# The output projection by seven products on halves, with six of eight blocks finished by an accumulating transfer

## The chip, the cores and the metric

The kernel runs on one core of one Trainium2 chip. The metric is the device time of one execution in microseconds, as the median over runs. The engines of the core are TensorE (PE, with its weight loads in a row of their own, PEld), VectorE (DVE), ScalarE (ACT), GpSimd (POOL) and SyncE (SP). SP and POOL issue the transfers: SP through a hardware queue (q1), POOL through a software queue (q0), which alone can add to what stands at the destination.

## The reference, cut to what matters

One layer on x of 1024 positions by 1024 channels, float32:

```
h = x @ w_in + b_in                       # -> xa, za, xb, zb, ga, gb
ya = RG_LRU(causal_conv4(xa)) * silu(za)
yb = MultiScalePool(xb) * silu(zb)
merged = sigmoid(ga) * (ya @ w_proj_a) + sigmoid(gb) * (yb @ w_proj_b)
y = merged @ w_out + b_out
out = LayerNorm(alpha * x + y, ln_gain, ln_bias)      # alpha = 2 ** 0.25
```

The last two lines are the output projection and the norm. The norm takes mean and variance over the 1024 channels of a position, multiplies with the gain and adds the bias.

## The kernel before, in words

Each float32 operand of a matmul is split into a high and a low part (`split`: a ScalarE copy to the matmul's type, and a DVE subtraction), and each product is three matmuls: high by high, high by low, low by high. A matmul takes 128 by 128 weights and 512 columns into one of eight PSUM banks (`bank`).

The stages follow one another: the input projection in 22 groups (`Group`, kinds A, B and G), then the merge (`steps`, seven products on halves for each of the branches a and b), then the output projection. The input projection and the merge already use seven products on halves of the operands instead of eight. The sums of halves that the merge needs are made in device memory (DRAM) by transfers of POOL: `summed` queues a copy of 1 MB and then adds (`add_to`), as jobs in a list, and `run_jobs` takes some jobs off that list after each group, behind a small POOL copy (`paced`) that waits for that group's seventh product. Names: t1 to t4 are sums of the branch results ya and yb (t1b is the first for branch b), p1 to p4 sums of weights (p1a to p4a, p1b to p4b). The merge reads them back through SP: xa1r, wa1r and so on are its raw operands for branch a, product 1; xb6r is branch b, product 6.

The output projection of before (lines 1338 to 1398) is plain: for each of eight blocks of 128 positions and each of two halves of 512 output channels, one bank takes eight inner blocks by three passes (`o_mm`); DVE adds the bank to z, which holds alpha * x + b_out (`o_evac`), and takes the statistics of each half (`bn_stats`). When both halves of a block are done, `o_norm` makes mean and variance, the root on ScalarE, and two DVE scalings for each half, the second of which also adds the bias of the norm, and SP stores the block. The last bank is cut into two pieces of 256 columns. `split_m` splits the merged operand as it becomes ready, `load_wo` and `cast_wo` bring the weights.

The order of each engine's instructions is not that of the code. `Plan` records all operations, gives each a due time from a cost and from who needs it, and lays them out by a simulated clock: PE and POOL keep the order of the code, DVE, ScalarE and SP take what is ready and due first (line 359 on), and hold an instruction back if a more urgent one comes soon (line 361). Every instruction is emitted by line 389, so the profile names this one line and is read by tile names.

Of the kernel before, what the change touches and what calls it, by code (L numbers as in the profile page):

```python
# [16 lines left out]
P = 128  # L17
# [144 lines left out]
class Plan:  # L162
# [22 lines left out]
    def add(self, name, eng, op, args, kw):  # L185
# [6 lines left out]
        t.ins = refs[1:] if t.outs else refs  # L192
        t.deps, t.users, t.new = set(), [], []
# [61 lines left out]
    def order(self):  # L255
# [26 lines left out]
        state = {"table": None, "SP": 0.0, "ACT": 0.0, "POOL": 0.0, "pe": 0}  # L282
# [17 lines left out]
        def begin(t, now):  # L300
# [4 lines left out]
            t.start = now  # L305
            free[t.eng] = now + t.time
# [21 lines left out]
        while done < len(T):  # L328
            moved = True
            while moved:  # L330
# [10 lines left out]
                for e in ("ACT", "DVE", "SP", "POOL"):  # L341
# [60 lines left out]
def layer_kernel(ctx: ExitStack, tc: tile.TileContext, xq, x, w_in, par, wg, w_pool, wpa, wpb, w_out, rows, out):  # L402
# [33 lines left out]

    HALF = [slice(0, H), slice(H, S)]
# [289 lines left out]
    def a_gates(c, xc, xh, xl, sz):  # L727
# [388 lines left out]
    for i in range(1, len(order)):  # L1116
# [51 lines left out]
        if i >= 2:  # L1168
            run_jobs(1 if kind == "A" else 2, i, g.t7)
# [63 lines left out]
    sums, mh, ml = {}, {}, {}  # L1233
    HOMES = {2: (kt, kt), 5: (kt, xt), 4: (xt, rt), 3: (xt, xt)}
# [4 lines left out]
    def split_m(j, d, h):  # L1239
        if d % 2 == 0:  # L1240
            for k, t in enumerate((mh, ml)):
                f = HOMES[j][k]
                t[d // 2, h] = f(f"m{k}{d}{h}", F32R) if f is not kt else f(f"m{k}{d}{h}", F32R).rearrange("p (g s) -> p g s", g=2)
        sign = 1.0 if d < KQ else -1.0
        A.mul(of(mh, d, h), of(sums, d, h), sign)
        V.scalar_tensor_tensor(of(ml, d, h), of(sums, d, h), sign, of(mh, d, h).bitcast(F32), ALU.mult, ALU.subtract)

    wo = {}

    raw_wo = {}  # L1250


    def load_wo(e, p):
        raw_wo[e, p] = kt(f"wor{e}_{p}").rearrange("p (k n) -> p k n", k=2)
        nc.sync.dma_start(raw_wo[e, p], w_out[2 * p * P:2 * (p + 1) * P, e * H:(e + 1) * H].rearrange("(k p) n -> p k n", p=P))

    def cast_wo(e, p):
        h, l = ((wt if e == 0 else xt)(f"wo{t}{e}_{p}") for t in "hl")
        split(raw_wo.pop((e, p)), h, l)
        for k in range(2):  # L1260
            wo[e, 2 * p + k] = (h[:, k, :], l[:, k, :])
# [20 lines left out]
    for i, (n, j) in enumerate(steps):  # L1282
# [10 lines left out]
        for g in range(KQ):  # L1293
# [17 lines left out]
            if (n, j) in DONE:  # L1311
# [11 lines left out]
                else:  # L1323
                    V.tensor_tensor(u, t, sgs[i][g], ALU.mult)
                    V.tensor_tensor(of(sums, d, h), of(sums, d, h), u, ALU.add)
                    split_m(j, d, h)
            if (n, j, g) in CASTS:
                with nc.within(SOON):
                    cast_wo(0, CASTS.index((n, j, g)))
        if (n, j) in (("a", 4), ("b", 1)):  # L1330
            for p in range(2):
                load_wo(0, p if n == "a" else p + 2)
# [5 lines left out]
    for p in range(KQ):  # L1338
        load_wo(1, p)
        cast_wo(1, p)  # L1340
    rb = []
    for i in range(3):
        t = xt(f"row{i}", F32, (P, S))
        nc.sync.dma_start(t, rows[i:i + 1, :].to_broadcast((P, D)))
        rb.append(t)
    b_row, g_row, be_row = rb
    zt, stats = [], []
    for s in range(NK):
        t = xt(f"z{s}", F32, (P, S))
        nc.sync.dma_start(t, x[s * P:(s + 1) * P, :])  # L1350
        V.scalar_tensor_tensor(t, t, ALPHA, b_row, ALU.mult, ALU.add)
        zt.append(t)
        stats.append(const.tile([P, 4 if s == NK - 1 else 2, 6], F32, name=f"stats{s}"))
    eps = const.tile([P, 1], F32, name="eps")
    nc.gpsimd.memset(eps, EPS)

    def o_mm(ps, s, e, ks, sl=slice(0, H)):
        for k in ks:
            wh, wl = (w[:, sl] for w in wo[e, k])
# [94 lines left out]
```

## Time and profile before

| | |
|---|---|
| median of three runs | 754.5 us (754.29 to 754.6) |
| profiled execution | 754.04 us |
| its span, first to last instruction | 752.2 us |
| PE busy | 742.5 us, 3308 matmuls |
| DVE busy | 598.4 us |
| ACT busy | 432.2 us |
| POOL busy | 54.5 us |
| granted TensorE clock, mean of the span | 0.997 |
| moved by q1, by q0 | 99.43 MB, 35.65 MB |

Durations of single DVE and ACT rows include some time in which the next one has already started; two rows in sequence are closer together than the first one's duration. A POOL transfer's row is its issue, not its landing.

### The profile page before, as it was taken

How to read it: one execution, taken by the hardware profiler on the slowest of the kernel's cores; microseconds unless marked ns; L12 is line 12 of the kernel's file. 1: busy time of each engine (PE TensorE's matmuls, PEld its weight loads, DVE VectorE, ACT ScalarE, POOL GpSimd, SP SyncE). 2: the span in 40 equal slices, each digit the busy share in tenths (PEclk: the TensorE clock that was granted, in tenths of full speed). 3: DMA queues.
4: the chain of work that ended last, by engine and by line, in shares of the span. 5: the costliest groups of instructions: out<-in, count | busy, mean ns of one | idle time of the engine just before them, and what ended most of it. 6: DMA issues, size and time to landing. Idle time of an engine off the chain costs nothing.

```text
span 752.2 us, 8755 instructions
## 1 busy us (share of the span) xinstructions
PE 742.5 (99%) x3308; PEld 608.6 (81%) x3308; DVE 598.4 (80%) x740; ACT 432.2 (57%) x556; POOL 54.5 (7%) x101
## 2 busy tenths in 40 slices
PE   9999999999999999999999999999999999999996
PEld 6887888888788878878888888888888888888885
DVE  7898695959595969699977768779958896977587
ACT  7676969597787777788665444465543654230000
POOL 0160010101010100010011001000000000000000
PEclk9999999999999999999999999999999999999998
DMA  9146567657566647254278526898599996181022
GB/s 343 64 145 156 179 159 198 166 175 195 147 163 198 166 176 173 85 171 142 80 161 171 112 76 176 309 382 270 197 300 302 330 295 220 57 315 48 29 93 103
DMA packets 54730, 135.90 MB, mean 181 GB/s; under 512 B 3936, under 2 KB 7136, under 8 KB 54624
## 3 DMA queue, kind: packets, MB, share of 16 engines
q1 hardware_dynamic: 41248, 99.43, 37.9%
q0 software_dynamic: 12896, 35.65, 21.4%
q8 instruction: 26, 0.43, 0.2%
q10 hardware_dynamic: 544, 0.26, 0.1%
q14 instruction: 16, 0.13, 0.1%
HBM read 114.36 MB, written 56.62 MB: 227 GB/s over the span
## 4 chain that ended last, share of the span: by engine, by line
PE 95%; ACT 2%; DVE 1%; DMA 1%; issue 0%; DVEq 0%; ACTq 0%
PE ps_o L389 12%; PE a_B L389 11%; PE a_A L389 10%; PE a_G L389 10%; PE pa_a L389 6%; PE pa_b L389 6%; PE c_A L389 6%; PE c_B L389 5%; PE c_G L389 4%; PE ps_pool L389 3%; PE pc_b L389 3%; PE pc_a L389 3%; PE e_A L389 3%; PE ps_s L389 3%; PE e_G L389 3%; PE e_B L389 3%
## 5 line engine op out<-in xcount | busy, mean ns | idle before, releaser
L389 PE MATMUL ps_o<-woh,m 128*128 128x512 f32 (+1 forms) x272 | 80.5, 379 | 0.0
L389 ACT ACT_TABLE_LOAD x39 | 50.0, 1283 | 42.8 <-DVE mv L389 40.1
L389 PEld LDWEIGHTS ps_o<-woh,m 128*128 128x128 f32 x272 | 50.1, 188 | 10.1
L389 PE MATMUL ps_o<-wol,m 128*128 128x512 f32 (+1 forms) x136 | 51.5, 378 | 0.0
L389 DVE TENSOR_TENSOR i<-i,xc 128x1024 f32<-128x1024 f32 x8 | 9.8, 1225 | 38.6 <-ACT i L389 38.6
L389 POOL COPY paced<-pace 128x1 f32<-128x1 f32 x19 | 13.4, 706 | 259.6 <-ACT pace L389 259.6
L389 DVE SCALAR_TENSOR_TENSOR xc<-xp,par_sb,xc 128x1024 f32<-128x1024 f32 x24 | 30.8, 1282 | 0.5
L389 PEld LDWEIGHTS ps_o<-wol,m 128*128 128x128 f32 x136 | 25.6, 188 | 5.0
L389 DVE TENSOR_TENSOR z<-ps_o,z 128x512 f32<-128x512 f32 (+1 forms) x17 | 11.2, 659 | 18.8 <-PE ps_o L389 18.3
L389 PE MATMUL pa_a<-oh,oh 128*128 128x512 f32 x64 | 24.9, 389 | 0.0
L389 PE MATMUL pa_a<-oh,ol 128*128 128x512 f32 x64 | 24.9, 389 | 0.0
L389 PE MATMUL pa_a<-ol,oh 128*128 128x512 f32 x64 | 24.9, 389 | 0.0
L389 PE MATMUL pa_b<-oh,oh 128*128 128x512 f32 x64 | 24.9, 389 | 0.0
L389 PE MATMUL pa_b<-ol,oh 128*128 128x512 f32 x64 | 24.9, 389 | 0.0
L389 PE MATMUL pa_b<-oh,ol 128*128 128x512 f32 x64 | 24.9, 389 | 0.0
L389 ACT ACTIVATE m<-m 128x512 fp32r<-128x512 f32 x16 | 10.1, 632 | 25.3 <-DVE m L389 25.3
L389 ACT ACTIVATE i<-ps_g,par_sb 64x512 f32<-64x512 f32 x32 | 21.9, 685 | 3.3 <-DVE r L389 2.8
L389 ACT ACTIVATE sd<-mv,eps 128x1 f32<-128x1 f32 x8 | 2.4, 295 | 34.9 <-DVE mv L389 34.9
L389 ACT ACTIVATE r<-ps_g,par_sb 64x512 f32<-64x512 f32 x32 | 21.9, 684 | 0.5
L389 ACT ACTIVATE zb<-zb,par_sb 128x1024 f32<-128x1024 f32 (+1 forms) x16 | 14.9, 937 | 10.7 <-DVE zb L389 10.3
L389 PE MATMUL c_B<-x64h,wd_B 128*128 128x512 f32 x64 | 21.0, 389 | 0.0
L389 PE MATMUL c_A<-x64h,wd_A 128*128 128x512 f32 x64 | 21.0, 389 | 0.0
(435 smaller groups left out, 2380.9 us busy)
## 6 DMA issues: line engine op xcount, KB each, us to landing
sg<-sg SPq DMA_DIRECT2D x16, 512.0 KB, 3.6
ra_A<-in_w_in SPq DMA_DIRECT2D x8, 512.0 KB, 4.9
rb_A<-in_w_in SPq DMA_DIRECT2D x8, 512.0 KB, 3.8
ya<-r SPq DMA_DIRECT2D x8, 512.0 KB, 2.9
ra_B<-in_w_in SPq DMA_DIRECT2D x8, 512.0 KB, 3.4
rb_B<-in_w_in SPq DMA_DIRECT2D x8, 512.0 KB, 3.7
yb<-zb SPq DMA_DIRECT2D x8, 512.0 KB, 6.0
sgla<-sg SPq DMA_DIRECT2D x8, 512.0 KB, 6.3
```

The costliest lines, as they stand in the source:

```text
L389: getattr(getattr(nc, t.op[0]), t.op[1])(*a, **k)
```

## The change

The output projection becomes seven products on halves: the sums of halves of the weights are made by POOL transfers in DRAM (`output_sums`), those of the merged operand by DVE in SBUF (`o_sums`, `o_sum4`), and z takes each product as it is finished (`o_add`), in the order 1, 6, 7, 5, 3 and then, block by block, 4 and 2. x plus b_out / alpha is made in DRAM by POOL transfers (`biased_input`). For blocks 0 to 6 the sum of a row comes from a second output of the two last adds and the sum of squares from a second output of Square on ScalarE; only block 7 keeps `bn_stats`. For blocks 0 to 5 the output in DRAM is preset with the bias of the norm, and the scaled block is added to it by a POOL transfer. `run_jobs` takes two or three jobs a group instead of one or two. The planner adds PE's present lag to a due time where it decides to hold an instruction back. Removed: the loops of the projection of before,

```diff
-    for s in range(NK):
-        ps = bank(f"ps_o{s}_0")
-        o_mm(ps, s, 0, range(NK))
-        o_evac(ps, s, 0, H)
-    for s in range(NK - 1):
-        ps = bank(f"ps_o{s}_1")
-        o_mm(ps, s, 1, range(NK))
-        o_evac(ps, s, H, D)
-        o_norm(s)
-    s = NK - 1
-    for w in (slice(0, H // 2), slice(H // 2, H)):
-        ps = bank(f"ps_o{s}_1_{w.start}")[:, 0:H // 2]
-        o_mm(ps, s, 1, range(NK), w)
-        o_evac(ps, s, H + w.start, H + w.stop)
-    o_norm(s)
```

`split_m`, the bias row and `o_mm`. Added, cut to its core:

```diff
--- before.py
+++ after.py
@@ -190,6 +190,9 @@
         out = args[0]
         t.outs = [out] if isinstance(out, Ref) else []
         t.ins = refs[1:] if t.outs else refs
+        if isinstance(kw.get("accum_out"), Ref):
+            t.ins = [r for r in t.ins if r is not kw["accum_out"]]
+            t.outs.append(kw["accum_out"])
...
-                        if any(u.due < t.due and when < end and u.due < end - HOLD for when, u in soon):
+                        if any(u.due < t.due and when < end and u.due + state["lag"] < end - HOLD for when, u in soon):
...
+    def output_sums():
+        a11, a12, a21, a22 = (w_out[H * k:H * (k + 1), H * i:H * (i + 1)].rearrange("(q p) n -> q p n", p=P)
+                              for i in range(2) for k in (1, 0))
+        p1 = summed("p1o", a21, a22)
+        p3 = summed("p3o", a11, a21)
+        p2 = summed("p2o", a11, p1)
+        src["w", "o"] = {1: a11, 2: a12, 4: a22, 5: p1, 6: p2, 7: p3, 3: summed("p4o", a12, p2)}
+
+
+    xb_d = [dram.tile([2 * P, D], F32, tag=f"xb{i}", name=f"xb{i}") for i in range(4)]
+    bias_d = dram.tile([1, D], F32, tag="bias", name="bias")
+
+    def biased_input():
+        for sl in HALF:
+            t = epool.tile([1, H], F32, tag="e", name=f"bias_{sl.start}")
+            nc.sync.dma_start(t, rows[0:1, sl])
+            A.mul(t, t, 1.0 / ALPHA)
+            nc.sync.dma_start(bias_d[:, sl], t)
+        for i in (2, 3, 0, 1):
+            jobs.append(lambda i=i: nc.gpsimd.dma_start(xb_d[i], x[2 * P * i:2 * P * (i + 1), :]))
+            jobs.append(lambda i=i: add_to(xb_d[i], bias_d.to_broadcast((2 * P, D))))
...
             input_sums1("a")
+            output_sums()
         elif c == NK - 1:
             input_sums2("a")
+            biased_input()
...
-            run_jobs(1 if kind == "A" else 2, i, g.t7)
+            run_jobs(3 if kind == "B" else 2, i, g.t7)
...
+    def o_first(d):
+
+        p, i = divmod(d - KQ, 2)
+        if i == 0:
+            om.setdefault(1, []).append([kt(f"o1{n}{p}", F32R).rearrange("p (g s) -> p g s", g=2) for n in "hl"])
+        high, low = (t[:, i, :] for t in om[1][p])
+        A.mul(high, of(sums, d, 1), -1.0)
+        V.scalar_tensor_tensor(low, of(sums, d, 1), -1.0, high.bitcast(F32), ALU.mult, ALU.subtract)
+
+    def o_sums(p):
+
+        b22, b12, b11 = sums[p, 0], sums[2 + p, 0], sums[2 + p, 1]
+        V.tensor_tensor(b11, b12, b11, ALU.subtract)
+        t2[p] = xt(f"t2o{p}", F32)
+        V.scalar_tensor_tensor(t2[p], b11, -1.0, b22, ALU.mult, ALU.subtract)
+        V.tensor_tensor(b12, b12, b22, ALU.add)
+
+    def o_sum4(p):
+
+        V.scalar_tensor_tensor(t2[p], t2[p], -1.0, sums[p, 1], ALU.mult, ALU.subtract)
...
+                    cast_wo(1 if k < 2 else 6, k % 2, wt)
...
+    O_STEPS = (1, 6, 7, 5, 3, 4, 2)
+    zt = {}
+    for s in (4, 5, 6, 7, 0, 1, 2, 3):
+        zt[s] = xt(f"z{s}", F32, (P, S))
+        nc.sync.dma_start(zt[s], xb_d[s // 2][(s % 2) * P:(s % 2 + 1) * P, :])
+    g_row, be_row = (xt(f"row{i}", F32, (P, S)) for i in (1, 2))
+    nc.sync.dma_start(g_row, rows[1:2, :].to_broadcast((P, D)))
+    nc.sync.dma_start(be_row, rows[2:3, :].to_broadcast((P, D)))
+
+    BY_DMA = (0, 1, 2, 3, 4, 5)
+    for s in BY_DMA:
+        nc.sync.dma_start(out[s * P:(s + 1) * P, :], rows[2:3, :].to_broadcast((P, D)))
+    acc = const.tile([P, 2 * NK], F32, name="o_acc")
...
+    def o_add(s, e, ps, sign, first, final, sl=slice(0, H)):
+        z = zt[s][:, e * H:(e + 1) * H][:, sl]
+        op = ALU.add if sign > 0 else ALU.subtract
+        if final and s != last:
+            V.scalar_tensor_tensor(z, z, ALPHA if first else 1.0, ps, ALU.mult, op, accum_out=acc[:, 2 * s + e:2 * s + e + 1])
+        elif first:
+            V.scalar_tensor_tensor(z, z, ALPHA, ps, ALU.mult, op)
+        else:
+            V.tensor_tensor(z, z, ps, op)
+        if final and s == last:
+            for k in (range(2) if sl == slice(0, H) else (sl.start // (H // 2),)):
+                i = 2 * e + k
+                V.bn_stats(stats[:, i, :], zt[s][:, i * H // 2:(i + 1) * H // 2])
...
+            nm, var = (const.tile([P, 1], F32, name=f"{n}{s}") for n in ("nm", "var"))
+            V.tensor_scalar(nm, acc[:, 2 * s:2 * s + 1], acc[:, 2 * s + 1:2 * s + 2], -1.0 / D, ALU.add, ALU.mult)
+            sq = kt(f"sq{s}")
+            A.activation(sq, zt[s], AF.Square, bias=nm, accum_out=var)
+            A.activation(sd, var, AF.Sqrt, bias=eps, scale=1.0 / D)
+            mean, op = nm, ALU.add
...
+        if s in BY_DMA:
+            A.mul(zt[s], zt[s], sd)
+            add_to(out[s * P:(s + 1) * P, :], zt[s])
+            return
...
+    def operands(j):
+        f, w = (xt, xt) if j == 2 else (kt, wt)
+        if j != 6:
+            for p in range(2):
+                load_wo(j, p, rt)
+            for p in range(2):
+                cast_wo(j, p, w)
+        o_input(j, f)
...
+    for i, j in enumerate(O_STEPS[:5]):
+        if j == 6:
+            for p in range(2):
+                o_sum4(p)
+        operands(O_STEPS[i + 2])
+        for g in range(KQ):
+            if j == 1:
+                a[g] = bank(f"oa_{g}")
+            elif j == 7:
+                c[g] = bank(f"oc_{g}")
+            ps = c[g] if j == 7 else a[g]
+            o_product(ps, j, g, j in (1, 7), j == 3)
+            if j == 1:
+                o_add(4 + g, 0, ps, 1, True, False)
+            elif j == 6:
+                o_add(4 + g, 1, ps, -1, True, False)
+            elif j == 7:
+                o_add(g, 1, ps, -1, True, False)
+            elif j == 5:
+                o_add(g, 1, ps, -1, False, True)
+            else:
+                o_add(g, 0, ps, 1, True, True)
+                o_norm(g)
+
+    for g in range(KQ):
+        o_product(c[g], 4, g, False, True)
+        o_add(4 + g, 1, c[g], -1, False, True)
+        pieces = (slice(0, H),) if g < KQ - 1 else (slice(0, H // 2), slice(H // 2, H))
+        for sl in pieces:
+            ps = bank(f"oe_{g}_{sl.start}")[:, 0:sl.stop - sl.start]
+            o_product(ps, 2, g, True, True, sl)
+            o_add(4 + g, 0, ps, 1, False, True, sl)
+        o_norm(4 + g)
```

Two places show how instructions stand.

POOL's queue from the last jobs of branch a to the sums of branch b, before (t4a, t1b, t3b, t2b, t4b are the DRAM sums of the merge's operands; ya and yb are the branch results in DRAM; `paced` is the pacing copy):

```order
L389 DMA t4a_2703<-ya_1057 512x512 x2
L389 COPY paced_601<-pace_595 128x1
L389 DMA t1b_3702<-yb_3408 512x512 x2
L389 COPY paced_601<-pace_595 128x1
L389 DMA t3b_3802<-yb_3408 512x512
L389 DMA t2b_3888<-t1b_3702 16x16384
```

And with the change, from the same t4a (xb0 to xb3 are the four DRAM tiles of x plus bias, two blocks of rows each):

```order
L394 DMA t4a_2185<-ya_1007 512x512 x2
L394 DMA xb2_3351<-in_x 16x16384
L394 COPY paced_613<-pace_610 128x1
L394 DMA xb2_3351<-bias_2805 256x2x512
L394 DMA xb3_3508<-in_x 16x16384
L394 DMA xb3_3508<-bias_2805 256x2x512
L394 COPY paced_613<-pace_610 128x1
L394 DMA xb0_3655<-in_x 16x16384
L394 DMA xb0_3655<-bias_2805 256x2x512
L394 DMA xb1_3810<-in_x 16x16384
L394 COPY paced_613<-pace_610 128x1
L394 DMA xb1_3810<-bias_2805 256x2x512
```

Four copies and four adds stand between the last t4a and the first t1b, which follows them behind one more pacing copy.

DVE at the end of the program, before (ps_o is a bank, z6 and z7 the last two blocks, row1 the gain, row2 the bias of the norm):

```order
L389 RECIPROCAL sd6_5883<-sd6_5883 128x1
L389 TENSOR_TENSOR z7_5429<-ps_o7_1_0_5866,z7_5429 128x256
L389 SCALAR_TENSOR_TENSOR z6_5427<-z6_5427,sd6_5883,row2_5409 128x512 x2
L389 BN_STATS stats7_5615<-z7_5429 128x6
L389 TENSOR_TENSOR z7_5429<-ps_o7_1_256_5900,z7_5429 128x256
L389 BN_STATS stats7_5615<-z7_5429 128x6
L389 BN_AGGR mv7_5933<-stats7_5615 128x2
```

And with the change (oc and oe are the banks of products 4 and 2, o_acc the row sums, nm the negative mean):

```order
L394 SCALAR_TENSOR_TENSOR z6_5273,o_acc_5642<-z6_5273,oe_2_0_5882 128x512
L394 TENSOR_SCALAR nm6_5905<-o_acc_5642 128x1
L394 SCALAR_TENSOR_TENSOR z6_5273<-z6_5273,nm6_5905,row1_5455 128x512 x2
L394 TENSOR_TENSOR z7_5279<-z7_5279,oc_3_5594 128x512
L394 RECIPROCAL sd6_5916<-sd6_5916 128x1
L394 SCALAR_TENSOR_TENSOR z6_5273<-z6_5273,sd6_5916,row2_5457 128x512
L394 TENSOR_TENSOR z7_5279<-z7_5279,oe_3_0_5921 128x256
L394 SCALAR_TENSOR_TENSOR z6_5273<-z6_5273,sd6_5916,row2_5457 128x512
L394 BN_STATS stats_5954<-z7_5279 128x6
L394 TENSOR_TENSOR z7_5279<-z7_5279,oe_3_256_5937 128x256
L394 BN_STATS stats_5954<-z7_5279 128x6 x3
L394 BN_AGGR mv7_5961<-stats_5954 128x2
```

Block 6's first scalings now stand in front of block 7's other half, and two of the statistics of that half stand behind the last add.

## Rows read from the trace of the kernel before

**Rows 1.** The page's first part: busy us, share of the span and instructions of each engine.

```profile
PE 742.5 (99%) x3308; PEld 608.6 (81%) x3308; DVE 598.4 (80%) x740; ACT 432.2 (57%) x556; POOL 54.5 (7%) x101
```

**Rows 2.** The chain of waits in order of time, its last piece on PE: start us, us, engine, tile and line.

```profile
656.42 88.34 PE ps_o L389 x408
```

**Rows 3.** The same chain, two stages of the merge: product 1 of branch a (pa_a) and product 6 of branch b (pa_b).

```profile
498.54 10.88 PE pa_a L389 x48
...
602.02 10.88 PE pa_b L389 x48
```

**Rows 4.** The timeline of PE in the last bank: start us, us, engine, line, operation, out<-in. Between these two rows stand two more of the same size.

```profile
739.34 0.28 PE L389 MATMUL ps_o<-wol,m 128*128 128x256 f32 x1
...
739.70 0.28 PE L389 MATMUL ps_o<-wol,m 128*128 128x256 f32 x1
```

**Rows 5.** The timeline of DVE where instructions stand back to back: six of 128x512, three of 128x1024.

```profile
659.73 3.70 DVE L389 SCALAR_TENSOR_TENSOR m<-m,m 128x512 fp32r<-128x512 f32 x6
663.34 3.49 DVE L389 TENSOR_TENSOR wol<-wor,woh 128x1024 fp32r<-128x1024 f32 x3
```

**Rows 6.** The timeline of DVE at the end.

```profile
744.79 0.42 DVE L389 TENSOR_TENSOR z<-ps_o,z 128x256 f32<-128x256 f32 x1 [0.55 <-PE ps_o L389]
745.25 0.43 DVE L389 BATCH_NORM_STATS2 stats<-z 128x6 f32<-128x256 f32 x1
745.71 0.26 DVE L389 BATCH_NORM_AGGREGATE mv<-stats 128x2 f32<-128x24 f32 x1
746.01 1.42 DVE L389 SCALAR_TENSOR_TENSOR z<-z,mv,row 128x512 f32<-128x512 f32 x2
...
747.53 1.41 DVE L389 SCALAR_TENSOR_TENSOR z<-z,sd,row 128x512 f32<-128x512 f32 x2
```

**Rows 7.** The tile view of the output: its stores, and from issue to landing.

```profile
L389 SPq DMA_DIRECT2D out<-z x16: 332/332/343, 710.4 to 749.0; - x16
...
DMA to landing us min/median/max: 2.0/2.0/4.1
```

**Rows 8.** Groups of instructions by form from 480 us on: engine, operation, tiles, shapes, count | busy us, mean ns of one | idle before.

```profile
L389 DVE TENSOR_TENSOR z<-ps_o,z 128x512 f32<-128x512 f32 x15 | 10.4, 692 | 18.3 <-PE ps_o L389 17.8
L389 DVE RECIPROCAL sd<-sd 128x1 f32<-128x1 f32 x8 | 1.3, 157 | 0.3 <-ACT sd L389 0.3
L389 ACT CAST woh<-wor 128x1024 fp32r<-128x1024 f32 x8 | 8.3, 1051 | 9.4 <-DVE ol L389 6.2 <-DMA wor<-in_w_out 3.2
L389 ACT ACTIVATE sd<-mv,eps 128x1 f32<-128x1 f32 x8 | 2.4, 295 | 34.9 <-DVE mv L389 34.9
L389 ACT ACTIVATE zb<-zb,par_sb 128x1024 f32<-128x1024 f32 x2 | 2.2, 1140 | 0.0
```

**Rows 9.** The timeline of POOL: issues of transfers, with the idle time before them and what ended it.

```profile
95.17 1.00 POOL L389 DMA_DIRECT2D p3a<-in_wpa  x1
95.82 1.01 POOL L389 DMA_DIRECT2D p2a<-in_wpa  x1
...
379.76 1.05 POOL L389 DMA_DIRECT2D t2a<-ya  x1 [45.91 <-DMA ya<-r]
...
411.81 1.02 POOL L389 DMA_DIRECT2D t4a<-ya  x1 [9.93 <-DMA t4a<-ya]
...
454.68 0.66 POOL L389 DMA_DIRECT2D t1b<-yb  x1 [17.54 <-issue]
...
474.28 0.49 POOL L389 DMA_DIRECT2D t4b<-t1b  x1
...
553.91 1.04 POOL L389 DMA_DIRECT2D t2b<-yb  x1 [79.13 <-DMA yb<-zb]
```

**Rows 10.** Transfers by line: KB each (where known), median us from issue to landing. p2b<-in_wpb is a copy of 1 MB, t4b<-t1b too, p3a has a copy and an add, t4a two adds.

```profile
p3a<-in_wpa POOLq DMA_DIRECT2D x2, 1024.0 KB, 8.4
...
t4a<-ya POOLq DMA_DIRECT2D x2, 1024.0 KB, 11.9
...
row<-in_rows SPq DMA_DIRECT2D x3, 512.0 KB, 8.6
...
p2b<-in_wpb POOLq DMA_DIRECT2D x1, 1024.0 KB, 6.1
...
t4b<-t1b POOLq DMA_DIRECT2D x1, 11.1
```

**Rows 11.** Two stretches: start and end, length, busy us of each engine with its instructions, granted clock, mean busy share of the DMA engines, GB/s.

```profile
560.00:609.00 49.00, 49.00 (x218) 40.58 (x217) 40.93 (x50) 21.22 (x26) 3.20 (x4) 1.00 1.07 304
489.00:508.00 19.00, 19.00 (x86) 15.73 (x85) 14.79 (x16) 12.29 (x14) 0.00 (x0) 1.00 1.03 383
```

**Rows 12.** Transfers by line, SP's loads in the first burst of the merge and while POOL adds.

```profile
wa1r<-in_wpa SPq DMA_DIRECT2D x2, 512.0 KB, 8.1
...
wb5r<-p1b SPq DMA_DIRECT2D x2, 512.0 KB, 17.2
```

**Rows 13.** The timelines of SP, ScalarE and DVE: issue, cast and low part of the second wa1r.

```profile
490.18 0.37 SPq L389 DMA_DIRECT2D wa1r<-in_wpa  x1
...
499.18 1.05 ACT L389 CAST oh<-wa1r 128x1024 fp32r<-128x1024 f32 x1 [4.65 <-DMA wa1r<-in_wpa]
...
500.26 1.23 DVE L389 TENSOR_TENSOR ol<-wa1r,oh 128x1024 fp32r<-128x1024 f32 x1 [0.94 <-ACT oh L389]
```

**Rows 14.** The timeline of DVE: low parts of xb6r.

```profile
587.86 2.35 DVE L389 TENSOR_TENSOR ol<-xb6r,oh 128x1024 fp32r<-128x1024 f32 x2
```

More of the change, by code (lines that the diff above doesn't have):

```diff
@@ L305, in begin @@
             t.start = now
+            if t.eng == "PE":
+                state["lag"] = now - ideal[t.i]
             free[t.eng] = now + t.time
@@ L1230, in load_sg @@
             sgs[i] += [t[:, 0, :], t[:, 1, :]]
-    sums, mh, ml = {}, {}, {}
-    HOMES = {2: (kt, kt), 5: (kt, xt), 4: (xt, rt), 3: (xt, xt)}
+    sums, t2 = {}, [None] * 2
     def of(t, d, h):
         return t[d // 2, h][:, d % 2, :]
[L1239 to L1261, printed above, removed]
+    om, ow = {}, {}
@@ new lines, in o_sum4, with o_input @@
+    def o_sum4(p):
+        V.scalar_tensor_tensor(t2[p], t2[p], -1.0, sums[p, 1], ALU.mult, ALU.subtract)
+    def o_input(j, f):
+        raws = {6: t2, 7: [sums[2 + p, 0] for p in range(2)], 5: [sums[2 + p, 1] for p in range(2)],
+                3: [sums[p, 0] for p in range(2)], 4: t2, 2: [sums[p, 1] for p in range(2)]}[j]
+        om[j] = []
+        for p in range(2):
+            h, l = (f(f"o{j}{n}{p}", F32R) for n in "hl")
+            if f is kt:
+                h, l = (t.rearrange("p (g s) -> p g s", g=2) for t in (h, l))
+            split(raws[p], h, l)
+            om[j].append((h, l))
@@ L1335, in layer_kernel @@
     merge.close()
[L1338 to L1347, printed above, removed]
-    for s in range(NK):
[L1349 to L1353, printed above, removed]
+    O_STEPS = (1, 6, 7, 5, 3, 4, 2)
@@ L1365, in o_evac @@
-    def o_evac(ps, s, lo, hi):
-        w = D // stats[s].shape[1]
-        nc.vector.tensor_tensor(zt[s][:, lo:hi], ps, zt[s][:, lo:hi], ALU.add)
-        for c in range(lo, hi, w):
-            nc.vector.bn_stats(stats[s][:, c // w, :], zt[s][:, c:c + w])
+    stats = const.tile([P, 4, 6], F32, name="stats")
+    last = NK - 1
+    def o_add(s, e, ps, sign, first, final, sl=slice(0, H)):
[11 more added lines that the diff above has]
+                V.bn_stats(stats[:, i, :], zt[s][:, i * H // 2:(i + 1) * H // 2])
@@ L1398, in layer_kernel, with o_product @@
-    o_norm(s)
+    def o_product(ps, j, g, start, stop, sl=slice(0, H)):
+        for q in range(KQ):
+            mh, ml = (t[:, q % 2, g * P:(g + 1) * P] for t in om[j][q // 2])
+            wh, wl = (t[:, q % 2, sl] for t in ow[j][q // 2])
+            for i, (l, r) in enumerate(((mh, wh), (mh, wl), (ml, wh))):
+                nc.tensor.matmul(ps, l, r, start=start and q == 0 and i == 0, stop=stop and q == KQ - 1 and i == 2,
+                                 skip_group_check=True)
+    def operands(j):
[6 more added lines that the diff above has]
+        o_input(j, f)
@@ new lines, in layer_kernel @@
+    a, c = ([None] * KQ for _ in range(2))
+    operands(6)
+    for i, j in enumerate(O_STEPS[:5]):
+        if j == 6:
+            for p in range(2):
+                o_sum4(p)
[15 more added lines that the diff above has]
+                o_add(g, 1, ps, -1, False, True)
+            else:
+                o_add(g, 0, ps, 1, True, True)
+                o_norm(g)
```

46 lines of the change are left out of this document (28 added, 18 removed).

## The prediction

> **What bounds the kernel now.** First the page's busy times: TensorE (PE) is busy 742.5 of 752.2 us, VectorE (DVE) 80%, ScalarE 57%; only PE is near the span [rows 1]. Then the chain of waits in order of time: its last long piece is the output projection, 408 matmuls in 88.34 us without a break, from 656.42 to 744.76 [rows 2], and behind it a DVE chain for the last block of rows up to the end [rows 6]. So time is won by PE columns not multiplied, or by a shorter tail; all else only has to stay off PE's path. The sum is made against the profiled execution, 754.04 us (span 752.2 and 1.84 around it), which is 0.46 below the median of 754.5.
>
> **Matmuls, the gain.** Before: 16 sums over eight blocks of the inner dimension, three passes each, 384 full products (the last sum is cut in two halves of 256 columns, hence 408 instructions). Now seven products on halves: 7 x 4 row groups x 4 inner blocks x 3 passes = 336, the last group again cut in two. 48 full matmuls take 10.88 us in the stages of the chain in front [rows 3], 0.227 each, and the halves follow each other by 0.12 [rows 4]. Now: 27 groups of 12 are 27 x 2.72 = 73.4, the last 24 halves 2.9, together 76.3: 12.0 less than 88.34. But 30 x 2.72 + 48 x 0.12 is only 87.4 for the old projection: 1.0 of its 88.34 is a pitch that was slightly longer, and that may come back. The gain is 11.0 to 12.0; I take 11.6.
>
> **Does DVE keep up inside the projection?** It now splits ten more weight tiles and twelve operand tiles, forms the half sums, and takes a bank out per product. In the order of the change there stand, from the first bank of product 1 to the last bank of product 5 (40.8 us of PE), 25 instructions of 128x1024 and 16 of 128x512. Back to back the former follow by 1.13 us and the latter by 0.61 [rows 5]: 28.3 + 9.8 = 38.0 us, 93% of PE's time. That hides, with little over; a bank is wanted again only three groups (8.2 us) after its product, which is the cover. Cost taken: 0. Without this cover a backlog of more than 8 us would go to PE one for one. ScalarE has 22 casts of about 1 us there and is no bound.
>
> **The tail, a loss.** Before, the tail is 7.4 us (744.78 to 752.2). The last 256 columns are added at 744.79, as soon as PE is done, and one row of statistics follows; DVE ends at 748.94 [rows 6], and the output lands 2.0 after its issue [rows 7]. In the order of the change DVE still has block 6 to finish there, behind a longer chain: two adds that also sum the row, the mean, Square over 1024 on ScalarE, its root, and only then the scaling. Let T be PE's end. Product 4 and the split product 2 of block 7 take 5.6, so block 6's last bank is ready at T-5.6. Add 0.69 and mean 0.2: T-4.6 with hand-overs. Square: the nearest row is a 1024-wide ScalarE instruction, 1.14 [rows 8]; T-3.4. Two scalings 1.42, add of block 7's other half 0.61, reciprocal 0.16, scaling 0.67, add 0.41, scaling 0.75, one bn_stats 0.4: T+1.0. Only now the last 256 columns: 0.41, then three bn_stats (two of them were left over from the other half) 1.25, aggregate 0.3: T+2.9, where before it stood at T+1.2. So +1.7 from the order alone.
> To this comes what no row shows: an instruction with a second output. It costs nothing (the lower end; no row would make it a gain) or up to a short instruction of its own: 0.16 (reciprocal) on DVE, 0.30 (root) on ScalarE [rows 8]. Block 6's chain has one of each, 0.45, and the blocks in front pass on about as much: their period (two adds 1.22 and their reads 0.3, mean 0.25, Square 1.14 and its read 0.3, hand-over of the root 0.2, two scalings 1.42, reciprocal 0.16) is 5.0 against PE's 5.44, so a lag from the norms of product 3 is worked off by only 0.4 a block. I take +0.9, together +2.6, bounds +1.0 to +7.
> (The Trainium skill, VectorE: DVE Perf Modes, "Two Vector instructions with no wait between them", says that an op which also writes its accumulator is two instructions, the second a read of it. The trace of before has no such op, so it neither agrees nor differs; by that rule the second outputs cost something, and at 0.16 and 0.30 for the reads the tail would be +2.2 without the blocks in front.)
>
> **Transfers through POOL.** Sixteen more jobs of 1 MB go into POOL's queue: eight for the sums of the output weights, paced behind groups well before the last ya is stored, where nothing waits for them, and eight for x plus bias. These last stand between t4a and t1b. POOL waits for ya until 379.76 anyway, issues its last t4a at 411.81 and is free at about 424 [rows 9, 10]. A pair is a copy (6 us) and an add (8.4 to 11.9, taken as 10) [rows 10]; a copy may ride beside the add in front (95.17 and 95.82 were issued 0.65 apart [rows 9]). Four pairs: 46 to 64 us. So t1b, issued at 454.68 before, comes at 470 to 488, and t4b<-t1b, landed at 474.28 + 11.1 = 485.4, lands at 501 to 519. Who waits? The next add, t2b<-yb, only starts when yb is stored, at 553.91 [rows 9]: 35 us to spare. But in 489 to 508 the merge fetches its first operands at 383 GB/s with POOL's queue idle; 560 to 609, with POOL adding, shows 304 in all [rows 11]. A 512 KB load lands in 17 us there, against 8.1 for the two of wa1r in the first burst [rows 12]. The tightest load of that burst is the second wa1r: issued 490.18, cast at 499.18, its low part ready at 501.49 [rows 13], while PE wants it two groups into the stage, at 498.54 + 5.44 = 503.98 [rows 3]: 2.5 us of margin. At 8 us later PE would stand for 5.5; at no delay for 0. I take 1.0, near the lower end, since POOL's dependent transfers leave gaps and only part of the window is shared.
> (The Trainium skill, DMA: Bandwidth & Descriptors, "Anatomy of one DMA — SWDGE (gpsimd) path", fits such a transfer as 2.0 us plus bytes over 436e3, an estimate of 4.4 us for 1 MB. By it the eight jobs take 35 us, t1b moves by 5, and the stall is 0. The rows show 6 and 8.4 to 11.9, and I go by them.)
> Presetting six output blocks with the bias (six loads of 512 KB on SP) and adding to them through POOL is hidden: block 5's add is issued about T-4 and a 1 MB add took at most 12. ScalarE's two multiplications of the bias, and the changed rule by which the planner holds instructions back, cost 0 by themselves; if they do not, PE shows new gaps between 300 and 350 us.
>
> **Sum.** 752.2 - 11.6 + 2.6 + 1.0 = 744.2 span, +1.84 = 746.0 for a profiled execution, +0.46 = 746.5 as a median.
>
> **Rivals.** (A) The norms take over: Square with its sum at 1.6 us instead of 1.14, or both second outputs at 0.3, bring a block's period to 5.4 or above, so nothing is worked off and the lag of the four norms of product 3 (each with 2.5 us of DVE and 2.8 of ScalarE in 2.72 of PE) stands in the tail: 3 to 7 more, 749 to 753. For it: the 93% above, and that DVE waits in order for ScalarE in every block. Against: 0.4 us of slack a block by the rows. (B) The merge stalls by the full 5.5 us, or at two places: 750 to 752. For it: 304 against 383 GB/s. Against: in 560 to 609 the same mixture cost PE nothing. (C) Slower than before: the add of one broadcast bias row is slow. The place is POOL's queue before t1b. With y us per add, t4b lands at 424 + 24 + 4y + 31, so t2b is late from y = 18.7; its split is ready at 590.2 [rows 14] and PE wants it at 602.0, so PE stalls from y = 21.7, four us for each further one, and the 8 us gained are gone at y = 24. At 30 it would be 780. For it: a broadcast row of 512 KB took 8.6 [rows 10], so twice that is 17, close to the edge. Against: that one stood behind other loads. (D) No lag and no stall: 743 to 744.
>
> **How the numbers follow.** Forecast (744.3 to 748.5) 0.60; A 0.17; B 0.13; C 0.05; D 0.05. The range, 743.0 to 752.5, takes in A and B. A difference of 0.2% (1.5 us) is about what a measurement of this kernel can tell from none. Faster: all but C and the far end of A, 0.93; same 0.02; slower 0.05.
>
> **What would show it.** The matmuls of the projection in the chain: 360 rows, 76 to 77.3 us in one piece. The tail: from the last matmul to the end 9 to 11 us, with three bn_stats behind the last add. The merge: a gap before the third group of its first product, and t1b issued between 465 and 490. Rivals: DVE rows with a wait for ScalarE's Square of 1.6 and adds of block 7 that start long after their banks (A); POOL adds of xb above 19 us (C). I am wrong if PE has gaps inside the projection, or if the tail stays at 7.4.

## The result, and the profile after

The changed kernel takes 748.57 us (median of 11 runs, 745.58 to 753.15), the kernel before 754.56 us beside it (11 runs, 753.78 to 758.6). The ratio is 0.9921 with a 95% interval of 0.9903 to 0.9939: faster by 0.8%. The profiled execution took 748.43 us with a span of 746.6, 5.6 less than before. The forecast was 746.5; the time lies inside the range of 743.0 to 752.5 and 0.07 above the likeliest case's own range. The sum came out 2 us too low: two losses and the gain were mis-sized, not all in the same direction, so part of the errors cancels, which is luck.

The first part of the page of the kernel after, which answers to [rows 1]:

```profile
PE 733.2 (98%) x3248; PEld 599.9 (80%) x3248; DVE 600.0 (80%) x746; ACT 457.4 (61%) x585; POOL 76.0 (10%) x125
```

PE has 60 instructions fewer (408 of the projection became 348) and is busy 9.3 us less. POOL has 24 instructions more. To see where 5.6 us come from, the chain of waits is cut at three places: the start of the merge, the start of the projection, the last matmul. The chain of the kernel after, start us, us, engine, tile:

```profile
487.50 2.52 PE e_B L394 x12
490.02 14.01 DMA wa1r<-in_wpa
...
504.06 1.05 ACT oh L394
...
505.13 1.24 DVE ol L394
...
506.42 6.86 PE pa_a L394 x22
513.27 10.88 PE pe_a L394 x48
...
660.26 22.32 PE oa L394 x96
682.57 11.18 PE oc L394 x48
693.75 22.27 PE oa L394 x96
716.02 2.77 PE oc L394 x12
```

Before, product 1 of branch a was one piece of 10.88 us [rows 3]. Now the chain leaves PE at 490.02 for the load of the second wa1r and comes back at 506.42. In the timeline of PE its first matmul starts at 498.22 and the first one behind it at 513.11: 14.89 us, 4.0 more (before, the same two stood at 498.37 and 509.25). From there to the projection nothing is lost: it starts 3.84 later than before (660.26 against 656.42), the 4.0 less the 0.15 by which the merge started earlier. The last matmul of the kernel after is this one, in the timeline of PE:

```profile
737.82 0.28 PE L394 MATMUL oe<-wo2h,o2l 128*128 128x256 f32 x1
```

So the projection takes 738.10 - 660.26 = 77.84 us where it took 88.34 [rows 2], a gain of 10.5, and PE has no gap in it. The tail is 746.6 - 738.10 = 8.5 where it was 7.44 (752.2 - 744.76). Together: 3.84 - 10.50 + 1.06 = -5.6, the whole difference.

What stands in the place where the 4.0 us went, in the timeline of PE (the idle time before an instruction in brackets, with what ended it):

```profile
503.43 0.39 PE L394 MATMUL pa_a<-oh,ol 128*128 128x512 f32 x1
505.15 0.50 PE L394 MATMUL pa_a<-oh,oh 128*128 128x512 f32 x1 [1.34 <-ACT oh L394]
505.50 0.39 PE L394 MATMUL pa_a<-ol,oh 128*128 128x512 f32 x1
506.42 0.63 PE L394 MATMUL pa_a<-oh,ol 128*128 128x512 f32 x1 [0.53 <-DVE ol L394]
506.84 0.63 PE L394 MATMUL pa_a<-oh,oh 128*128 128x512 f32 x1
...
509.83 0.49 PE L394 MATMUL pa_a<-ol,oh 128*128 128x512 f32 x1
510.16 0.39 PE L394 MATMUL pa_a<-oh,ol 128*128 128x512 f32 x1
```

and in the same stretch cut in three (start and end, length, busy us of each engine with its instructions, granted clock, DMA share, GB/s):

```profile
503.00:506.40 3.40, 1.55 (x6) 0.65 (x4) 1.23 (x1) 2.00 (x2) 0.39 (x1) 1.00 1.45 592
506.40:510.00 3.60, 3.58 (x9) 2.83 (x10) 2.36 (x2) 1.99 (x2) 0.00 (x0) 0.53 1.06 429
510.00:513.00 3.00, 3.00 (x15) 2.50 (x14) 0.00 (x0) 0.00 (x0) 0.00 (x0) 0.99 0.49 185
```

There are two losses, one behind the other. First PE waits, for the cast and then for the low part of the late tile: from 503.43 to 506.42 it starts three matmuls in 2.99 us instead of 0.68, 2.3 us lost. Then, though its operands are there, eight matmuls take from 506.42 to 509.83, 0.427 each instead of 0.227: another 1.6 us. In that stretch the granted clock is 0.53, the lower of its two levels (1.2 GHz) for nearly all of it; right behind it is 0.99. The waits in brackets alone, 1.87 us, would give less than half of the loss.

The timeline of POOL shows why the load was late, and answers to [rows 9]:

```profile
405.30 0.91 POOL L394 DMA_DIRECT2D xb<-in_x  x1
...
420.54 1.56 POOL L394 DMA_DIRECT2D xb<-bias  x1 [13.04 <-DMA xb<-in_x]
421.47 1.17 POOL L394 DMA_DIRECT2D xb<-in_x  x1
...
469.53 2.35 POOL L394 DMA_DIRECT2D t1b<-yb  x1
487.38 1.03 POOL L394 DMA_DIRECT2D t1b<-yb  x1 [15.51 <-DMA t1b<-yb]
488.02 1.06 POOL L394 DMA_DIRECT2D t3b<-yb  x1
...
502.90 0.50 POOL L394 DMA_DIRECT2D t4b<-t1b  x1
```

The pairs of copy and add for x plus bias follow by some 16 us, so t1b goes out at 469.53 instead of 454.68 [rows 9], and its add and t3b are in flight from 487.4 to beyond 500, just when SP fetches the first operands of the merge. The transfers by line between 486 and 500, after (queue, packets, MB, share of 16 engines; then KB each and us from issue to landing):

```profile
q1 hardware_dynamic: 1389, 2.92, 61.0%
q0 software_dynamic: 567, 1.24, 44.0%
...
wa1r<-in_wpa SPq DMA_DIRECT2D x1, 512.0 KB, 14.0
```

and before, the same stretch:

```profile
q1 hardware_dynamic: 2363, 5.04, 98.7%
...
wa1r<-in_wpa SPq DMA_DIRECT2D x1, 512.0 KB, 9.0
```

SP's queue (q1) moved 5.04 MB in these 14 us before and 2.92 MB after: POOL's queue (q0) took 1.24 MB, and the sum fell too, from 5.04 to 4.17 MB. This agrees with the Trainium skill, DMA: Bandwidth & Descriptors, "Queues, rings and completion order", by which each DMA engine takes turns between the queues that have work for it. The fall of the sum it does not tell. The count takes an add once (sixteen transfers of 1 MB, eight of them adds, raise POOL's queue by 16.78 MB in e12_jobs_early, against the kernel before), so whether an add's reading of what stands at its destination fills the gap is open.

The tail, in the timeline of DVE, answers to [rows 6]:

```profile
732.52 0.69 DVE L394 SCALAR_TENSOR_TENSOR z<-z,oe 128x512 f32<-128x512 f32 x1 [1.12 <-PE oe L394]
733.13 0.08 DVE L394 DVE_READ_ACCUMULATOR z<-z,oe 128x1 f32 x1
733.25 0.21 DVE L394 TENSOR_SCALAR nm<-o_acc 128x1 f32<-128x1 f32 x1
734.83 1.42 DVE L394 SCALAR_TENSOR_TENSOR z<-z,nm,row 128x512 f32<-128x512 f32 x2 [1.37 <-ACT sq L394]
...
737.95 0.74 DVE L394 SCALAR_TENSOR_TENSOR z<-z,sd,row 128x512 f32<-128x512 f32 x1
...
738.95 0.40 DVE L394 TENSOR_TENSOR z<-z,oe 128x256 f32<-128x256 f32 x1
739.27 1.07 DVE L394 BATCH_NORM_STATS2 stats<-z 128x6 f32<-128x256 f32 x3
740.38 0.26 DVE L394 BATCH_NORM_AGGREGATE mv<-stats 128x2 f32<-128x24 f32 x1
```

Block 6 starts as soon as its bank is there (DVE stands for PE before it, 1.12 us), waits 1.37 us for Square, and pushes the last 256 columns of block 7 to 738.95, 0.85 behind the last matmul. Before, they were added 0.03 behind it.

### The profile page after: what moved, and what is told of

Its sections match the earlier page's. It is cut to its first block, busy times and chain, and to the rows that moved or that the text cites. A ratio compares the mean times of both kernels' runs of the same rounds, so it can differ in the third digit from the quotient of the medians.

```text
span 746.6 us, 8782 instructions
## 1 busy us (share of the span) xinstructions
PE 733.2 (98%) x3248; PEld 599.9 (80%) x3248; DVE 600.0 (80%) x746; ACT 457.4 (61%) x585; POOL 76.0 (10%) x125
## 4 chain that ended last, share of the span: by engine, by line
PE 95%; DMA 3%; DVE 1%; ACT 0%; DVEq 0%; ACTq 0%; issue 0%
PE a_A L394 11%; PE a_G L394 10%; PE a_B L394 10%; PE oa L394 6%; PE pa_b L394 6%; PE c_B L394 6%; PE c_A L394 6%; PE pa_a L394 5%; PE c_G L394 5%; PE ps_pool L394 3%; PE pc_b L394 3%; PE pc_a L394 3%; PE e_A L394 3%; PE ps_s L394 3%; PE oc L394 3%; PE e_G L394 3%
## 5 line engine op out<-in xcount | busy, mean ns | idle before, releaser
L394 PE MATMUL ps_pool<-mixh,wp 128*128 128x512 f32 x64 | 20.6, 394 | 0.0
L394 POOL DMA_DIRECT2D out<-z x6 | 7.1, 1190 | 124.7 <-ACT z L394 124.7
L394 PE MATMUL e_B<-x,wah_B 128*128 128x512 f32 x64 | 19.7, 389 | 0.0
L394 PE MATMUL e_A<-x,wah_A 128*128 128x512 f32 x64 | 19.7, 389 | 0.0
L394 PE MATMUL c_G<-x64h,wd_G 128*128 128x512 f32 x56 | 18.4, 389 | 0.0
L394 DVE TENSOR_TENSOR_SCAN r<-a,i 128x1024 f32<-128x1024 f32 x8 | 18.3, 2283 | 0.1
L394 PE MATMUL e_G<-x,wah_G 128*128 128x512 f32 x56 | 17.2, 389 | 0.0
## 6 DMA issues: line engine op xcount, KB each, us to landing
xb<-bias POOLq DMA_DIRECT2D x4, 1024.0 KB, 12.6
```

The lines of the kernel that those rows point to most:

```text
L394: getattr(getattr(nc, t.op[0]), t.op[1])(*a, **k)
```

## Experiments

All are compared with runs of the kernel before on the same chip (754.26 to 754.43 us median).

**The transfers earlier: e1_early_xb.** The eight jobs for x plus bias go into POOL's queue ahead of t2a and t4a.

```diff
             output_sums()
+            biased_input()
         elif c == NK - 1:
             input_sums2("a")
-            biased_input()
...
-            run_jobs(3 if kind == "B" else 2, i, g.t7)
+            run_jobs(3 if i >= 10 else 2, i, g.t7)
```

> The kernel after, with the eight transfers that form x plus bias put ahead of the input sums t2a and t4a in POOL's queue instead of between t4a and t1b; nothing is left out. Theory (the jobs push t1b and the following into the merge's first loads, and PE stops twice and then runs 8 matmuls at half clock): the stand of 2.3 us before pa_a and most of the 0.63 us matmuls go, the projection starts near 656.3 instead of 660.3, and the time is 744 to 745.5. Rival (the merge's late operand has another cause, such as the planner's new rule or ScalarE's order): the stall stays and so does 748.5. Second rival: t2a and t4a, now 64 us later in the queue, are late themselves and PE stands before 500, then it is above 750.

Measured: 744.46 us (743.82 to 745.58), ratio 0.9871 (0.9856 to 0.9885). The chain of this kernel has product 1 of the merge in one piece again, and t1b goes out at 456.47:

```profile
499.51 10.88 PE pa_a L394 x48
...
657.38 22.32 PE oa L394 x96
```

The theory holds: 4.1 us come back in the medians, product 1 takes the 10.88 us of the kernel before, and the rivals (another cause of the late operand; t2a and t4a late in their turn) fall. In the profiled execution only 2.9 us show where the projection starts, because the merge starts 1.3 us later than in the kernel after (499.51 against 498.22): near the start of the program nine matmuls take 4.0 us (7.01 to 10.99) where the kernel after takes 2.2 (7.45 to 9.63), long before POOL's first transfer at 56.67. The spread shrinks from 7.6 us (11 runs) to 1.8 (4 runs), which fits a loss that hangs on how transfers meet, though only one execution of each kernel was profiled.

**The transfers alone: e2_jobs_alone.** The kernel before, with `output_sums` and `biased_input` added at the places of the change; the projection stays the old one.

```diff
             input_sums1("a")
+            output_sums()
         elif c == NK - 1:
             input_sums2("a")
+            biased_input()
...
-            run_jobs(1 if kind == "A" else 2, i, g.t7)
+            run_jobs(3 if kind == "B" else 2, i, g.t7)
```

> The kernel before, with the sixteen transfers of the change (the half sums of the output weights and x plus bias) added to POOL's queue at the same places; nothing reads what they make, and the projection is the old one. Theory (the transfers alone cost the merge its first loads): PE stands in front of the merge's first product and its clock falls behind it, the projection starts 3 to 4 us later and the time is 757.5 to 758.5. Rival (the stall comes from the new arithmetic or the planner's rule, not from the transfers): 754 to 755, no stop near 505.

Measured: 766.94 us (764.97 to 770.97), ratio 1.017 (1.013 to 1.0209): 12.5 us slower, three times what the theory gave. The place is the one expected, in the chain of this kernel:

```profile
491.65 23.82 DMA wa1r<-in_wpa
...
515.50 1.05 ACT oh L389
...
516.60 1.22 PE pa_a L389 x2
```

PE stands 11.1 us for that cast, and the 24 matmuls from it to the end of product 1 take 7.7 us instead of 5.4. So the transfers alone make the loss, and the rival falls; but the size of the loss is not fixed by the transfers. POOL issued the add of t1b and t3b at nearly the same times as in the kernel after (486.09 and 486.73), yet the load took 23.8 us instead of 14.0. SP's last load of xa6r went out 2.1 us ahead of it here (489.53) and 6.2 us ahead of it in the kernel after (483.83), so more stood in front of it; whether that makes the difference was not tried.

**The same, early: e12_jobs_early.** e2_jobs_alone with the jobs for x plus bias ahead of t2a and t4a, by the edit of e1_early_xb.

```diff
             output_sums()
+            biased_input()
         elif c == NK - 1:
             input_sums2("a")
-            biased_input()
...
-            run_jobs(3 if kind == "B" else 2, i, g.t7)
+            run_jobs(3 if i >= 10 else 2, i, g.t7)
```

> e2_jobs_alone with the eight transfers for x plus bias put ahead of t2a and t4a, as in e1_early_xb; nothing reads what the sixteen transfers make. Theory (the 12.5 us of e2_jobs_alone come from where the transfers stand, in front of the merge's first loads): 754 to 755.2, as the kernel before. Rival (sixteen more MB of transfers cost time wherever they stand, by bandwidth): 757 or above.

Measured: 754.33 us (753.6 to 756.5), ratio 1.0006 (0.9997 to 1.0015). Sixteen more transfers of 1 MB cost nothing where nobody waits for what they slow down. Its chain has pa_a at 501.32 and ps_o at 659.20, the 157.88 us of the kernel before. That its merge starts 2.8 us later than before is a matter of the first 20 us, in which PE starts 56 matmuls instead of 68.

**The transfers behind: e3_xb_behind.** The jobs for x plus bias behind t1b, t3b and t4b.

```diff
             input_sums2("a")
-            biased_input()
...
             input_sums1("b")
+            biased_input()
```

> The kernel after, with the x plus bias transfers put behind t1b, t3b and t4b in POOL's queue, so that they run between about 440 and 560; nothing is left out. Theory (any POOL transfer in 485 to 505 slows the merge's first loads): wa1r still takes about 14 us and the time stays at 747.5 to 749.5. Rival (it is t1b, t3b and t4b in particular that hurt, by the dependency or by the rows that they read): wa1r back to about 8 us, the stall gone, 744 to 745.5.

Measured: 759.75 us (757.49 to 760.2), ratio 1.0066 (1.005 to 1.0081). Against what was expected, something is left out: in this kernel four transfers behind the jobs (one of t3b, two of t4b, one of t2b) were not issued any more, so parts of the input sums of branch b are left out; PE's work is unchanged. t1b goes out at 454.53 as before, and still the chain goes through a late load in front of the merge, and through a second one later in it:

```profile
489.60 18.72 DMA wa1r<-in_wpa
...
522.65 19.13 DMA wa3r<-p4a
```

Both numbers expected are missed, but not the question: it is not t1b and t3b in particular. An add and a copy for x plus bias were issued at 489.53 and 490.47 here, the next pair at 507.44 and 508.36, and they slow the merge's loads as well.

**One more block by transfer: e4_seven_by_dma.** Block 6 also gets its bias by transfer, so two scalings leave DVE's tail.

```diff
-    BY_DMA = (0, 1, 2, 3, 4, 5)
+    BY_DMA = (0, 1, 2, 3, 4, 5, 6)
```

> The kernel after, with block 6 also getting its bias by transfer, so that its two scalings of 1.42 us in all leave DVE's tail (they go to one multiplication on ScalarE, as for blocks 0 to 5); nothing is left out. Theory (DVE's queue sets the tail): the end comes 1.0 to 1.4 us earlier, 747.2 to 747.5. Rival (block 6's add by POOL, issued about 736 and 5.9 or more to land, sets the end): no change or up to 1 us later, 748.5 to 749.5.

Measured: 747.85 us (747.04 to 749.95), ratio 0.9918 (0.9902 to 0.9934), between the two ranges expected, and the run to run spread of the kernel after cannot tell it from that kernel. The profile can: the last matmul ends at 737.26, the span at 745.2, so the tail is 7.9 instead of 8.5. DVE ends 1.3 us nearer to the last matmul; the rest went to the last stores. The tile view of the output (transfers, count, duration; then the landing):

```profile
L394 POOL DMA_DIRECT2D out<-z x7: 1179/1191/1262, 712.9 to 737.6; - x7
L394 SPq DMA_DIRECT2D out<-z x2: 350/354/357, 740.9 to 741.5; - x2
```

The transfers by line give 2.7 us for these two stores, against 2.0 in the kernel after: they stand beside POOL's add for block 6, issued at 737.62.

**Both: e10_early_seven.** The edits of e1_early_xb and e4_seven_by_dma.

```diff
-    BY_DMA = (0, 1, 2, 3, 4, 5)
+    BY_DMA = (0, 1, 2, 3, 4, 5, 6)
...
+            biased_input()
         elif c == NK - 1:
             input_sums2("a")
-            biased_input()
```

> e1_early_xb and e4_seven_by_dma together; nothing is left out. Theory (two separate costs, the stall in front of the merge and two scalings in DVE's tail): 744.46 less the 0.7 that e4_seven_by_dma showed, 743.3 to 744.2, a ratio of 0.985 to 0.987. Rival (with PE done earlier, block 6's add by POOL ends last): 744.5 to 745.5.

Measured: 743.85 us (743.24 to 748.35), ratio 0.9876 (0.9855 to 0.9897). Not to be told from e1_early_xb alone. In its profile the tail is 743.5 - 735.15 = 8.35, and the last stores take 3.1 us: what DVE saves the stores lose.

**No bias by transfer: e5_no_dma.** On top of e1_early_xb.

```diff
-    BY_DMA = (0, 1, 2, 3, 4, 5)
+    BY_DMA = ()
```

> e1_early_xb with no block's bias added by transfer: DVE scales with the bias for blocks 0 to 6 as it does for 6 and 7 there, ScalarE's scaling and the presets go; nothing is left out. Theory (DVE's queue carries the tail and has little over): each of six blocks costs DVE 1.4 us more, a block's period goes from about 5.0 to 5.9 against PE's 5.44, and the tail grows by 2 to 5 us: 746.5 to 749.5. Rival (the norms have slack enough, the transfers buy nothing): 744 to 745.

Measured: 747.84 us (746.35 to 750.36), ratio 0.9926 (0.9906 to 0.9946): 3.4 us more than e1_early_xb. PE's last matmul ends at 733.71 and the span at 744.6, a tail of 10.9 us instead of 8.6, and the chain runs through DVE and Square from 703 us on. So this part of the change is worth 2.3 (profile) to 3.4 us (medians), and the seven products without it give back up to a third of their gain.

**Statistics by DVE: e6_bn.** On top of e1_early_xb, cut to its core.

```diff
-        if final and s == last:
+        if final:
+            if s != last:
+                V.bn_stats(stats[s][:, e, :], zt[s][:, e * H:(e + 1) * H])
+                return
...
-        if s == last:
+        if True:
             mv = const.tile([P, 2], F32, name=f"mv{s}")
-            V.bn_aggr(mv, stats)
+            V.bn_aggr(mv, stats[s])
```

> e1_early_xb with the statistics of blocks 0 to 6 taken by bn_stats and bn_aggr on DVE, as block 7 has them, instead of the second outputs of the adds and of Square on ScalarE; nothing is left out. Theory (DVE stands 1.37 us for Square in every block, so DVE work of about that length is nearly free, and reads of 0.08 and 0.19 us cost little): a block's period stays near 4.6 us, block 6's chain gets about 0.5 us shorter, 743.5 to 744.8. Rival (DVE at 93% in the products 1 to 5 has no room for eight more bn_stats of about 0.6 us each): a lag of 2 to 5 us stands in the tail, 746 to 749.

Measured: 744.11 us (743.26 to 745.0), ratio 0.9863 (0.9846 to 0.9879). In its profile the last matmul ends at 735.16 and the span at 743.2: 8.0 instead of 8.6. Its DVE timeline, where a block no longer waits for Square:

```profile
729.58 0.69 DVE L394 TENSOR_TENSOR z<-z,oe 128x512 f32<-128x512 f32 x1 [0.97 <-PE oe L394]
730.30 0.69 DVE L394 BATCH_NORM_STATS2 stats<-z 128x6 f32<-128x512 f32 x1
731.03 0.21 DVE L394 BATCH_NORM_AGGREGATE mv<-stats 128x2 f32<-128x12 f32 x1
731.27 1.41 DVE L394 SCALAR_TENSOR_TENSOR z<-z,mv,row 128x512 f32<-128x512 f32 x2
```

The mean is in hand 1.66 us behind the start of block 6's add, where Square released the scaling 2.31 us behind it (734.83 - 732.52) in the kernel after. DVE still stands for PE's bank, so it had room: the second outputs on ScalarE buy nothing here, and the rival of a lag falls.

**Why the matmuls of the projection are slow: e8_kpad and e11_o2wt.** Both on top of e1_early_xb. The first lays the tiles of the pool kt at distances of 4608 bytes instead of 4160, in nine buffers; the second only puts product 2's weights in the weights' pool.

```diff
-NWORK = 10
+NWORK = 9
+KW = 1152
...
-        return kpool.tile([P, w], dt, tag="k", name=name)
+        return kpool.tile([P, KW], dt, tag="k", name=name)[:, 0:w]
```

> e1_early_xb with the tiles of the pool kt laid 4608 bytes apart instead of 4160, in nine buffers instead of ten; nothing is left out. Question: why the matmuls of products 1, 3, 4, 5, 6 and 7 follow each other by 0.230 to 0.233 us and those of product 2 and of the merge by 0.2267. Theory one (their stationary operand lies in kt, whose tiles start at other offsets than those of the pools of 4096 bytes): with tiles at multiples of 512 bytes the pitch falls to 0.227 and the projection from 77.9 to 76.4 us. Theory two (the moving operand in the weights' pool, or something else): 0.230 to 0.233 as before. One buffer fewer may cost time elsewhere, so only the pitch is read.

```diff
-        f, w = (xt, xt) if j == 2 else (kt, wt)
+        f, w = (xt, wt) if j == 2 else (kt, wt)
```

> e1_early_xb with the split weights of product 2 in the weights' pool instead of the pool xt; its input stays in xt; nothing is left out. Theory one (the stationary operand in kt makes the pitch longer): product 2 stays at 0.227 us. Theory two (the moving operand in the weights' pool does): product 2 goes to 0.230 or above.

Measured, one run each: 750.26 and 743.84 us. The chain of e8_kpad:

```profile
451.44 5.44 PE ps_pool L395 x24
...
663.60 21.76 PE oa L395 x96
685.36 10.88 PE oc L395 x48
```

21.76 / 96 is 0.2267 us, where the kernel after has 22.32 / 96 = 0.2325, and the projection takes 739.91 - 663.60 = 76.3 us. In e11_o2wt the groups of product 2 keep 2.72 to 2.74 us with their weights in the weights' pool, whose tiles are 4096 bytes apart like those of xt. So theory two falls, and the longer pitch goes with the pool kt. In the projection it is the stationary operand that lies there. But a moving operand in kt does the same, which neither experiment was made to ask: ps_pool, a stage in front, has its stationary operand (wp) in the weights' pool and its moving one (mixh, mixl) in kt. Its four pieces of 24 matmuls take 5.53 to 5.59 us in the kernel after, 0.230 to 0.233 each, and 5.44 (0.2267) in e8_kpad. One of them in the chain of the kernel after, which answers to the first line above:

```profile
443.64 5.59 PE ps_pool L394 x24
```

Most of what e8_kpad loses (its merge starts at 505.84, 6.3 us later than that of e1_early_xb) stands in front of ps_g, where PE waits 4.8 us for sg; e11_o2wt, with ten buffers, has no such wait. A version with ten buffers at the new distance was not tried.

## Why the prediction was right, and where its terms were wrong

**What bounds the kernel**: right. Every us of the difference stands on PE's path or behind its last matmul, and the cuts of the chain add up to the difference without a rest.

**Matmuls, 11.6 forecast, 10.5 measured**: the count was right, the pitch not, and 10.5 is below the forecast's own lower bound of 11.0. (The "360 rows" among its signs is a slip: its sum has 27 groups of 12 and 24 halves, the 348 that ran.) 76.7 us were forecast, which took the 0.227 of the merge for the new operands; e8_kpad shows that this is what they take in tiles 4608 bytes apart (76.3), and that 1.5 us of the 77.84 come from where the pool kt puts them. The prediction saw that 1.0 of the old 88.34 was a longer pitch, and took it for something that might or might not come back. That it goes with operands in kt only the experiment showed. The kernel before also kept part of the merged operand in kt, but whether the old 1.0 had the same cause was not tried.

**DVE keeps up, cost 0**: right. PE has no gap in the projection, and DVE waits for banks in the last blocks.

**The tail, +2.6 forecast, +1.06 measured**: right in its sign and in its order, too large; at 8.5 us it is also under the 9 to 11 given as a sign. The order alone was worked out to put the last 256 columns at T+1.0 (T is PE's end); even with the second outputs they stand at T+0.85. DVE's last two scalings start 4.10 us behind the last matmul instead of 2.77, 1.33 later, and the end of the program follows them 0.27 sooner, for a reason that was not looked into. The reads are 0.08 us on DVE and 0.18 to 0.19 on ScalarE (rows DVE_READ_ACCUMULATOR and ACTIVATION_READ_ACCUMULATOR), not 0.16 and 0.30, and the lag handed on by the blocks in front, about half of the +0.9, is zero: DVE is ready before block 6's bank. The trace agrees with the rule that was weighed (the Trainium skill, VectorE: DVE Perf Modes, "Two Vector instructions with no wait between them"): the accumulator's read has a row of its own. e6_bn adds that the second outputs were not the cheaper way.

**Transfers through POOL, +1.0 forecast, +4.0 measured**: this is the term that failed. Its mechanism was right to the tile: t1b later by 15 us, the second wa1r as the first operand to be late, a gap before the third group of the first product. That t1b's 469.53 is so close to the forecast 470 to 488 is in part luck. The first copy went out at 405.30, beside the last add of t4a, and not at 424. And the four pairs took 64 us, the upper end of 46 to 64, because each copy is issued about 1 us behind the add in front of it and then takes 14.7 us beside it, not 6. The value was chosen near the lower end of 0 to 5.5 because "only part of the window is shared"; the load took 14.0 us instead of 9.0 (8.1 is the middle of the two in [rows 12]). Less the forecast's 2.5 us of margin that is a stand of 2.5, and 2.3 was measured. But the bound had no term for the clock: 1.6 us of the loss are matmuls at the lower level after PE had stood. e2_jobs_alone shows that the upper end of 5.5 was no bound either. By the fit that the prediction cited beside its rows (the Trainium skill, DMA: Bandwidth & Descriptors, "Anatomy of one DMA — SWDGE (gpsimd) path", an estimate of 4.4 us for 1 MB) there would have been no stall. The xb copies took 14.7 and the adds 12.6 in the transfers by line, so the measurement decides against it here.

**Presets, adds to the output, the planner's rule, cost 0**: right. The adds to the output land 5.9 us after their issue and the last one is issued at 732.98; PE has no wait between 300 and 480, where before it had one of 0.6 us for ps_g.

**The rivals.** What happened lies between the forecast and B (the merge stalls fully), with B's place and three quarters of its price. A (the norms take over) did not happen in the kernel after, and e5_no_dma shows what it looks like when DVE gets 1.4 us more a block: 3.4 us. C (slow broadcast adds) needed 24 us an add; they took 12.6. D did not happen.

In the span the sum was 2.4 us too low: 3.0 for the stall and 1.1 for the pitch, less 1.5 for the tail and 0.15 for the front of the program. Without the tail's error it would have been 3.9: that the median lies only 2 us from the forecast is luck in that measure.

## What to carry to other kernels

Where a queue gets more jobs, ask not only who waits for them but what they will then run beside: two transfers of 1 MB, 15 us later than before, cost 4 us here and 12 in another kernel, and sixteen of them, put where no load was tight, cost nothing. When a burst of loads has 2 us of margin, move the jobs rather than estimate the collision. And a PE that stands can cost more than the wait in brackets: look at the length of the matmuls behind it.

## What the runs showed of the hardware that was not expected

- After standing 1.34 and 0.53 us, PE ran eight matmuls at 0.427 us each instead of 0.227, in a stretch with a granted clock of 0.53, and was back at 0.227 when the clock was at 0.99. Not every stand does this: in the same execution PE stood 1.64 us before 7.45, and the nine matmuls from there took 2.2 us at a granted clock of 1.00.
- Matmuls of 512 columns follow by 0.2267 us with their operands in tiles 4096 or 4608 bytes apart, and by 0.229 to 0.233 where the stationary operand (projection) or the moving one (ps_pool) lies in tiles 4160 bytes apart: 1.5 us in the projection. Both spacings that are fast are multiples of 512 bytes; which distance is needed was not tried.
- A hardware load of 512 KB beside two POOL transfers of 1 MB took 14.0, 18.7 and 23.8 us in three kernels, against 9.0 without them, and in the first of them the DMA engines moved less in sum by the profile's count (4.17 MB against 5.04 in 14 us).
- The last stores of the output, 256 KB each, land 2.0 us after their issue, and 2.7 to 3.1 beside an add by POOL.
